# Attention scores: stores of 4 MB in 32 KB runs, 64-column matmul tiles, and eight small stores from 64 partitions

## The chip, the cores and the metric

The kernel runs on one core of a Trainium2 chip; the other cores of the chip run nothing of this program. The metric is the device time of one execution in microseconds (us). Times are medians of runs in the fast state unless said otherwise. "End" times inside a run are us from the start of the profiled span; the measured time is some 1.9 us longer than the span.

## The reference, cut to what matters

```python
def setup_inputs():
    batch, heads, seq, dim = 8, 8, 512, 64
    ... # q, k: float32 [8, 8, 512, 64]
def reference(q, k):
    scale = 1.0 / np.sqrt(q.shape[-1])
    return np.einsum('bhqd,bhkd->bhqk', q, k) * scale   # float32 [8, 8, 512, 512]
```

16.8 MB are read and 67.1 MB written, so this is a kernel that writes.

## The kernel before

A unit is two batches. Its inputs come in two loads of 2 MB, are cast to bf16, transposed on TensorE, and sorted into `kT` and `qz`. `qz` holds the stationary operand of two heads, zero where the other head's rows are, so one matmul of 128 rows and 128 columns makes 64 query rows of two heads. Eight query rows make a tile of 2 MB, 16 KB contiguous in memory for each partition:

```python
RO = 8
out_r = out.rearrange("(v b) (n h) (u i) k -> v (b n) (h u) (i k)", b=2, h=2, i=RO)
...
def scores(v, n):
    kT, qz = ts[v]
    o = out_pool.tile([P, RO, S], f32, name="o")            # 4 buffers
    for i in range(0, RO, 2):
        ps = psum_pool.tile([P, 2, S], f32, name="ps")
        for w in range(2):
            nc.tensor.matmul(out=ps[:, w, :], lhsT=qz[:, i + w, n, :], rhs=kT[:, n]..., ...)
        evacuate(o[:, i:i + 2, :], ps)                      # ScalarE and VectorE in turn
        yield
    nc.sync.dma_start(out=out_r[v, n], in_=o...)            # 32 of these
```

## Time and profile before

| | before |
|---|---|
| time, median of 4 runs | 204.16 us (204.10 to 204.36) |
| span of the profiled run | 202.3 us |
| data packets | 5120 of 16 KB |
| data queue busy, share of 16 DMA engines | 97.7% |
| landing marks of the last store, sixteen engines | mean 198.53 us, last 201.01 us |

Every DMA engine that takes part in a transfer writes one mark of 4 bytes when its share has landed, and the packet records of the trace show the sixteen marks of the last store. The kernel is over when the last of them is, so the mean tells how much work there was and the distance from the mean to the last tells how unevenly it ended. (The prediction reads the same marks from the semaphore's records, which lie about 0.5 us later.)

### The profile page before, as it was taken

How to read it: one execution, taken by the hardware profiler on the slowest of the kernel's cores; microseconds unless marked ns; L12 is line 12 of the kernel's file. 1: busy time of each engine (PE TensorE's matmuls, PEld its weight loads, DVE VectorE, ACT ScalarE, POOL GpSimd, SP SyncE). 2: the span in 40 equal slices, each digit the busy share in tenths (PEclk: the TensorE clock that was granted, in tenths of full speed). 3: DMA queues.
4: the chain of work that ended last, by engine and by line, in shares of the span. 5: the costliest groups of instructions: out<-in, count | busy, mean ns of one | idle time of the engine just before them, and what ended most of it. 6: DMA issues, size and time to landing. Idle time of an engine off the chain costs nothing.

```text
span 202.3 us, 1549 instructions
## 1 busy us (share of the span) xinstructions
PE 106.1 (52%) x512; PEld 50.2 (25%) x512; DVE 129.6 (64%) x133; ACT 102.5 (51%) x130; POOL 26.8 (13%) x20
## 2 busy tenths in 40 slices
PE   0045557755854755858575575656564677642000
PEld 0034424432211322423222233223121222210000
DVE  6875669987765686878787788777544455553000
ACT  2254457967654448484756666574833344442000
POOL 1037775756000000000000000000000000000000
PEclk9999999978799699797979787896969655695555
DMA  6999999999999999999999999999999999999991
GB/s 214 428 441 428 424 441 421 424 395 434 437 421 434 432 423 431 434 428 428 437 424 431 431 424 434 434 428 431 434 428 428 431 434 428 428 437 429 416 447 75
DMA packets 5768, 83.99 MB, mean 415 GB/s; under 512 B 640, under 2 KB 640, under 8 KB 640
## 3 DMA queue, kind: packets, MB, share of 16 engines
q1 hardware_dynamic: 5760, 83.89, 97.7%
q8 instruction: 4, 0.07, 0.1%
q14 instruction: 4, 0.03, 0.0%
HBM read 16.78 MB, written 67.11 MB: 415 GB/s over the span
## 4 chain that ended last, share of the span: by engine, by line
DMA 52%; ACT 13%; DVE 13%; PE 10%; issue 2%; ACTq 0%; DVEq 0%; SPq 0%
DMA out_dram<-o 52%; ACT o L62 6%; DVE o L64 5%; PE ps L134 5%; ACT qz L99 4%; DVE qz L89 3%; ACT kT L99 3%; PE tp L120 3%; DVE kT L99 3%; PE tp L111 2%; DVE xb L83 1%; DVE qz L99 1%; ACTq L62 0%; DVEq L64 0%; SPq L140 0%
## 5 line engine op out<-in xcount | busy, mean ns | idle before, releaser
L134 PE MATMUL ps<-kT,qz 128*128 128x512 bf16 x256 | 87.3, 470 | 52.4 <-ACT o L62 43.3
L64 DVE TENSOR_SCALAR o<-ps 128x1024 f32<-128x1024 f32 x64 | 78.2, 1225 | 44.1 <-DMA out_dram<-o 28.5
L62 ACT ACTIVATE o<-ps 128x1024 f32<-128x1024 f32 x64 | 63.5, 1022 | 64.3 <-DMA out_dram<-o 50.9
L134 PEld LDWEIGHTS <-qz 128*128 128x128 bf16 x256 | 28.6, 115 | 98.6 <-issue 87.2
L83 POOL CAST xb<-xf 128x2048 bf16<-128x2048 f32 x14 | 26.1, 1893 | 21.5 <-DMA xf<-in_q_dram 18.1
L99 DVE COPY kT<-tp 64x512 bf16<-64x512 bf16 x32 | 22.0, 687 | 4.3 <-PE tp L111 3.8
L99 DVE COPY qz<-tp 64x512 bf16<-64x512 bf16 x32 | 22.0, 687 | 4.2 <-PE tp L120 3.7
L111 PE MATMUL tp<-identity,xb 128*128 128x128 bf16 x128 | 13.0, 267 | 17.0 <-DVE xb L83 11.1
L99 ACT COPY kT<-tp 64x512 bf16<-64x512 bf16 x32 | 18.5, 578 | 5.0 <-PE tp L111 4.7
L99 ACT COPY qz<-tp 64x512 bf16<-64x512 bf16 x32 | 18.5, 577 | 4.2 <-PE tp L120 3.9
L120 PE MATMUL tp<-identity,xb 128*128 128x128 bf16 x128 | 13.3, 271 | 8.1 <-ACT qz L99 4.9
L111 PEld LDWEIGHTS <-xb 128*128 128x128 bf16 x128 | 11.2, 122 | 21.3 <-ACT xb L83 11.1
L120 PEld LDWEIGHTS <-xb 128*128 128x128 bf16 x128 | 11.5, 123 | 12.6 <-issue 9.7
L89 DVE MEMSET qz<- 64x2048 uint32 x4 | 7.1, 1765 | 2.6 <-issue 1.4
L83 ACT CAST xb<-xf 128x2048 bf16<-128x2048 f32 x1 | 1.9, 1898 | 6.7 <-DMA xf<-in_k_dram 6.7
L83 ACT ACT_TABLE_LOAD x1 | 1.3, 1283 | 0.7 <-PEq L181 0.7
L83 DVE CAST xb<-xf 128x2048 bf16<-128x2048 f32 x1 | 1.2, 1227 | 0.0
masks.py:199 POOL TENSOR_SCALAR_AFFINE_SELECT identity<-identity 128x128 bf16<-128x128 bf16 x1 | 0.3, 292 | 0.1
masks.py:197 POOL MEMSET identity<- 128x128 bf16 x1 | 0.2, 205 | 0.3 <-POOLq L181 0.3
L181 POOL MEMSET const-float32-0.0<- 128x1 f32 x1 | 0.1, 98 | 0.2 <-issue 0.2
L181 POOL MEMSET const-bfloat16-1.0<- 128x1 bf16 x1 | 0.1, 101 | 0.0
L181 POOL MEMSET const-uint8-127<- 128x1 uint8 x1 | 0.1, 101 | 0.0
(1 smaller groups left out, 0.1 us busy)
## 6 DMA issues: line engine op xcount, KB each, us to landing
out_dram<-o SPq DMA_DIRECT2D x32, 2048.0 KB, 16.1
xf<-in_k_dram SPq DMA_DIRECT2D x4, 2048.0 KB, 11.3
xf<-in_q_dram SPq DMA_DIRECT2D x4, 2048.0 KB, 12.3
```

Source lines behind the costliest of these rows:

```text
L62: pinned(nc.scalar.mul(out=dst, in_=src, mul=scale))
L64: pinned(nc.vector.tensor_scalar(out=dst, in0=src, scalar1=scale, scalar2=None, op0=mybir.AluOpType.mult))
L83: pinned(copy(out=xb[:, :, s, :], in_=xf[:, s].rearrange("p (j d) -> p j d", j=J)))
L89: nc.vector.memset(qz[half(h), :, :, (1 - h) * U:(2 - h) * U], 0.0)
L99: pinned(copy(out=dst(s, h), in_=src[:, h]))
L111: pinned(nc.tensor.transpose(out=tp[:, j, :], identity=identity, in_=kb[:, j0 + j].rearrange("p s d -> p (s d)")))
L120: pinned(nc.tensor.transpose(out=tp[:, i, jj, :], identity=identity, in_=qb[:, RO * jj + i0 + i].rearrange("p s d -> p (s d)")))
L134: pinned(nc.tensor.matmul(out=ps[:, w, :], lhsT=qz[:, i + w, n, :], rhs=kT[:, n].rearrange("d m s j -> d (m s j)"), start=True, stop=True))
L181: nc = _bacc.Bacc("TRN2", target_bir_lowering=False, num_devices=1)
```

## The change

The intent, as the design suggests: fewer and longer packets (32 KB instead of 16 KB), and an evening-out of the sixteen DMA engines at the end. A tile now holds 16 query rows, 4 MB, of four heads. A matmul now makes 64 output rows (two heads, 32 of them each), so two of them, in the two 64-column halves of TensorE's array, fill the 128 partitions. They are called split matmuls or column tiles below. Inputs and outputs share three buffers. Two of the sixteen rows of one tile are computed on partitions 0 to 63 instead and leave in eight small stores, each of 8 partitions.

```diff
-    RO = 8
+    RO = 16
+    out_r = out.rearrange("(v b) (t h) (u i) k -> v (b t) (h u) (i k)", b=2, h=4, i=RO)
+    out_l = out.rearrange("(v b) (t x h) (u i) k -> v (b t) (h u) x (i k)", b=2, x=2, h=2, i=RO)
-    raw_pool ... bufs=3          out_pool ... bufs=4
+    big_pool = ctx.enter_context(tc.tile_pool(name="big", bufs=3))
+    LOW = 2
+    low_at = (1, 0)
+    low = low_pool.tile([D, 2, LOW, S], f32, name="low")
...
+    def store_low(n):
+        p0 = 32 * (n // 4) + n % 4
+        p = slice(p0, p0 + 29, 4)
+        nc.sync.dma_start(out=out_l[low_at + (p, slice(None), slice((RO - LOW) * S, RO * S))],
+                          in_=low[p].rearrange("p x i k -> p x (i k)"))
...
+            if (v, t) == low_at and i == RO - LOW:
+                for x in range(2):
+                    ps = psum_pool.tile([P, 2, S], f32, name="ps")
+                    for w in range(2):
+                        matmul(v, t, i + w, x, ps[half(0), w, :])
+                    evacuate(low[:, x], ps[half(0)])
...
             for w in range(2):
+                for x in range(2):
+                    matmul(v, t, i + w, x, ps[half(x), w, :])
...
+        nc.sync.dma_start(out=out_r[v, t], in_=src)
+        since = (v - low_at[0]) * TILES + t - low_at[1] - 1
+        if 0 <= since < 8:
+            store_low(since)
```

Cut: the casts of the first unit move from VectorE and ScalarE to GpSimd, and the order in which transposes are mixed in changes.

More of the change, by code (lines that the diff above doesn't have):

```diff
@@ L36 @@
     IW = 8 // JJ
+    TILES = N // 2
     f32 = mybir.dt.float32
@@ L42 @@
     k_r = k.rearrange("(v b) g (m j) d -> v (b g m) (j d)", b=2, j=R)
-    out_r = out.rearrange("(v b) (n h) (u i) k -> v (b n) (h u) (i k)", b=2, h=2, i=RO)
+    out_r = out.rearrange("(v b) (t h) (u i) k -> v (b t) (h u) (i k)", b=2, h=4, i=RO)
+    out_l = out.rearrange("(v b) (t x h) (u i) k -> v (b t) (h u) x (i k)", b=2, x=2, h=2, i=RO)
     consts = ctx.enter_context(tc.tile_pool(name="consts", bufs=1))
-    raw_pool = ctx.enter_context(tc.tile_pool(name="raw", bufs=3))
-    bf_pool = ctx.enter_context(tc.tile_pool(name="bf", bufs=5))
+    big_pool = ctx.enter_context(tc.tile_pool(name="big", bufs=3))
+    bf_pool = ctx.enter_context(tc.tile_pool(name="bf", bufs=6))
     t_pool = ctx.enter_context(tc.tile_pool(name="t", bufs=2))
-    out_pool = ctx.enter_context(tc.tile_pool(name="out", bufs=4))
+    low_pool = ctx.enter_context(tc.tile_pool(name="low", bufs=1))
     tpsum_pool = ctx.enter_context(tc.tile_pool(name="tpsum", bufs=2, space=bass.MemoryType.PSUM))
@@ L60, in evacuate @@
         nonlocal n_evac
-        if n_evac % 2 == 0:
+        if n_evac % 6 in (0, 2, 3):
             pinned(nc.scalar.mul(out=dst, in_=src, mul=scale))
@@ L71, in load_and_cast @@
     def load_and_cast(v):
+        xf = big_pool.tile([P, 2, 2, J * D], f32, name="big")
         both = []
-        for src in (k_r, q_r):
-            xf = raw_pool.tile([P, 2, J * D], f32, name="xf")
-            nc.sync.dma_start(out=xf, in_=src[v])
+        for x, src in enumerate((k_r, q_r)):
+            nc.sync.dma_start(out=xf[:, x], in_=src[v].rearrange("p (s c) -> p s c", s=2))
+        for x in range(2):
             xb = bf_pool.tile([P, J, 2, D], bf16, name="xb")
             for s in range(2):
-                if v == 0 and src is k_r:
-                    copy = (nc.vector.tensor_copy, nc.scalar.copy)[s]
-                else:
-                    copy = nc.gpsimd.tensor_copy
-                pinned(copy(out=xb[:, :, s, :], in_=xf[:, s].rearrange("p (j d) -> p j d", j=J)))
+                pinned(nc.gpsimd.tensor_copy(out=xb[:, :, s, :],
+                                             in_=xf[:, x, s].rearrange("p (j d) -> p j d", j=J)))
             both.append(xb)
         return both
-    def clear(qz, h):
-        nc.vector.memset(qz[half(h), :, :, (1 - h) * U:(2 - h) * U], 0.0)
     def rearrange(tp, pattern, dst):
@@ L125, in transpose, with matmul, scores @@
                                  .rearrange("d i n (m s jj) -> d s i n m jj", s=2, jj=JJ)[:, s])
-    def scores(v, n):
+    def matmul(v, t, i, x, dst):
         kT, qz = ts[v]
-        o = out_pool.tile([P, RO, S], f32, name="o")
-        for i in range(0, RO, 2):
+        pinned(nc.tensor.matmul(out=dst, lhsT=qz[:, i, 2 * t + x, :],
+                                rhs=kT[:, 2 * t + x].rearrange("d m s j -> d (m s j)"),
+                                start=True, stop=True))
+    def store_low(n):
[3 more added lines that the diff above has]
+                          in_=low[p].rearrange("p x i k -> p x (i k)"))
+    def scores(v, t):
+        o = big_pool.tile([P, RO, S], f32, name="big")
+        for i in range(0, RO, 2):
+            if (v, t) == low_at and i == RO - LOW:
[4 more added lines that the diff above has]
+                    evacuate(low[:, x], ps[half(0)])
+                yield
+                break
             ps = psum_pool.tile([P, 2, S], f32, name="ps")
             for w in range(2):
-                pinned(nc.tensor.matmul(out=ps[:, w, :], lhsT=qz[:, i + w, n, :],
-                                        rhs=kT[:, n].rearrange("d m s j -> d (m s j)"),
-                                        start=True, stop=True))
+                for x in range(2):
+                    matmul(v, t, i + w, x, ps[half(x), w, :])
             evacuate(o[:, i:i + 2, :], ps)
@@ L139, in scores @@
         src = o.rearrange("p i k -> p (i k)")
-        nc.sync.dma_start(out=out_r[v, n], in_=src)
+        if (v, t) == low_at:
+            nc.sync.dma_start(out=out_r[v, t, :, :(RO - LOW) * S], in_=src[:, :(RO - LOW) * S])
+            return
+        nc.sync.dma_start(out=out_r[v, t], in_=src)
+        since = (v - low_at[0]) * TILES + t - low_at[1] - 1
+        if 0 <= since < 8:
+            store_low(since)
     def take(steps, count):
@@ L147 @@
     make_identity(nc, identity)
-    qzs = [consts.tile([P, RO, N, P], bf16, name=f"qz{n}") for n in range(2)]
+    qzs = [consts.tile([P, RO, N, 2 * U], bf16, name=f"qz{n}") for n in range(2)]
     for qz in qzs:
-        for h in range(2):
-            clear(qz, h)
+        nc.vector.memset(qz, 0.0)
     cast = [load_and_cast(v) for v in range(UNITS)]
@@ L158 @@
         ahead = transpose(v + 1, *cast[v + 1]) if v + 1 < UNITS else iter(())
-        per_step = 3 if v == 0 else 1
-        for n in range(N):
-            take(ahead, 1)
-            for _ in scores(v, n):
-                take(ahead, per_step)
+        for t in range(TILES):
+            for n, _ in enumerate(scores(v, t)):
+                take(ahead, 1 + (n % 4 == 3) if v else 2 * (t > 0))
         for _ in ahead:
```

## The prediction

> **What bounds the kernel now.** I read the page from the top. The busy line, the slices and the queue come first, because they tell whether any engine has to be argued about at all.
>
> ```profile
> PE 106.1 (52%) x512; PEld 50.2 (25%) x512; DVE 129.6 (64%) x133; ACT 102.5 (51%) x130; POOL 26.8 (13%) x20
> ...
> DMA  6999999999999999999999999999999999999991
> ...
> DMA packets 5768, 83.99 MB, mean 415 GB/s; under 512 B 640, under 2 KB 640, under 8 KB 640
> ...
> q1 hardware_dynamic: 5760, 83.89, 97.7%
> ```
>
> No compute engine is over 64%, while the DMA digits are 9 in 38 of 40 slices, and the data queue alone is busy for 97.7% of sixteen engines' span. So the end is set by bytes divided by rate, plus the two edges (the 6 in front, the 1 at the end). Of 5760 packets 640 are under 512 B: 40 transfers times 16, the marks of landing. The other 5120 carry 83.89 MB, so 16 KB each: one run of a partition. Their time is 0.977 x 202.3 x 16 / 5120 = 618 ns on average.
>
> Next the waits and the chain, to see whether the queue ever ran dry.
>
> ```profile
> ACT o L62 <- DMA out_dram<-o: 50.9, 24, 3.0
> PE ps L134 <- ACT o L62: 43.3, 29, 2.4
> DVE o L64 <- DMA out_dram<-o: 28.5, 24, 2.0
> ```
>
> ScalarE waits 50.9 us and VectorE 28.5 us for a store to free an output buffer: compute is ahead and is held back by the stores. The chain of waits calls 52% DMA; its ACT, DVE and PE pieces are only the refill of a buffer while other stores are already queued.
>
> Last the windows over both edges (columns after the engines: clock, DMA share, GB/s):
>
> ```profile
> 0.00:2.00 2.00, 0.00 (x0) 0.00 (x0) 0.78 (x1) 1.27 (x1) 0.70 (x6) 1.00 0.54 98
> 2.00:4.00 2.00, 0.00 (x0) 0.00 (x0) 1.53 (x2) 0.01 (x1) 0.00 (x0) 1.00 0.60 205
> ...
> 40.00:42.00 2.00, 0.61 (x3) 0.19 (x2) 1.96 (x3) 1.77 (x3) 2.00 (x2) 1.00 1.04 360
> ...
> 196.00:197.00 1.00, 0.00 (x0) 0.00 (x0) 0.00 (x0) 0.00 (x0) 0.00 (x0) 0.50 0.92 393
> 197.00:198.00 1.00, 0.00 (x0) 0.00 (x0) 0.00 (x0) 0.00 (x0) 0.00 (x0) 0.50 0.84 360
> 198.00:199.00 1.00, 0.00 (x0) 0.00 (x0) 0.00 (x0) 0.00 (x0) 0.00 (x0) 0.50 0.27 115
> 199.00:200.00 1.00, 0.00 (x0) 0.00 (x0) 0.00 (x0) 0.00 (x0) 0.00 (x0) 0.50 0.15 66
> 200.00:201.00 1.00, 0.00 (x0) 0.00 (x0) 0.00 (x0) 0.00 (x0) 0.00 (x0) 0.50 0.04 16
> ```
>
> The end is a taper of 4 us. The sixteen marks of the last store's landing in the trace say the same: nine lie at 197.98 to 198.41 us, then 198.98, 199.32, 199.37, 199.41, 199.54, 200.61 and 201.48. One engine works 3 us longer than most. The second loss is 40 to 42 us, where loads give way to stores: 360 instead of 430 GB/s, some 0.3 us.
>
> **What the Trainium skill says.** (1) "DMA: Bandwidth & Descriptors", section "Why small descriptors are slow (HBM only)": a packet costs its 32-byte beats plus about 3 cycles. The trace agrees in size only: a 2 MB transfer takes about 2.097 MB / 430 GB/s = 4.88 us, 8 packets for each engine, and no larger packet is there to compare. (2) Same page, "The descriptor swizzle": in a transfer of 128 partitions, engines 0 to 7 serve partitions 0 to 63 and engines 8 to 15 the others. This profile does not tell engines apart. (3) Same page, "Why a DMA increments its semaphore by 16 and not by 1": a transfer whose slowest dimension is 8 goes to the lowest-numbered 8 engines. No run here shows it yet. (4) "TensorE: Matmul & The Clock Gate", Part 3: matmuls whose outputs lie in different column groups run at the same time; 3 such tiles were measured at 2.38 times. The kernel before has none.
>
> **The change, part by part.**
>
> *Longer runs.* 32 stores of 2 MB become 15 of 4 MB, one of 3.5 MB and 8 of 64 KB. Per engine the stores were 256 packets of 16 KB and become about 128 of 32 KB. By (1), 3 of 515 cycles are overhead in a 16 KB packet (512 beats + 3) and 3 of 1027 in a 32 KB one, a gain of 0.29%. Stores are 67.1 MB / 430 GB/s = 156 us, so an estimate of 0.45 us. There are also 8 full-width store marks fewer on engines 0 to 7 and 16 fewer on engines 8 to 15 (the 8 small stores use only half the engines); a mark took 9 ns in the packet records, so 0.1 us. Together 0.5 to 0.6 us, on the bound.
>
> *The small stores.* Two of 16 rows of one 4 MB tile are 512 KB. Stored in full width they would be 32 KB for each engine. They are moved to partitions 0 to 63 and stored 8 partitions at a time, so by (2) and (3) engines 0 to 7 take 64 KB each and the others none. Engines 8 to 15 lose 32 KB, engines 0 to 7 gain 32 KB: at 611 ns for 16 KB (the median packet) 1.2 us each way. If the late seven are among engines 8 to 15, which I take from the design of the change, the latest goes from 201.48 to about 200.3, and the early eight from at most 198.4 to 199.7: the end is 1.2 us earlier. A perfect levelling could give some 2.7 us (spread the shares after 197 evenly: the work is done near 198.2 instead of 201).
>
> *TensorE.* 256 matmuls of 128 columns become 512 of 64. In the trace, starts of 128x512 matmuls lie 0.427 us apart at half clock and 0.215 at full. If a pair overlaps, nothing changes (about 110 us). If it does not, a 4 MB tile takes 32 x 0.215 = 6.9 us at full clock plus two transpose groups of 0.5 us: 7.9 us, still below the 9.75 us of its store; at half clock 13.7 + 2 would exceed it[...].
>
> *VectorE and ScalarE.* The same 64 + 64 evictions in all but 2 of half height; ScalarE gets half as before. The transposes' copies stay 64 and 64. Per unit of 16 MB of output VectorE needs 16 x 1.225 + 16 x 0.687 = 30.6 us against 39 us of store: beside the path.
>
> *Buffers.* Inputs and outputs now share three buffers of 32 KB a partition. A tile fills in about 8 us, and may begin when the store three back has landed, while two more (19.5 us) are queued: 9 us of slack even with 2 to 3 us of late landing. The danger is the first tile. It takes the buffer of unit 1, whose casts on GpSimd (1.89 us each, all 16 there now) end about 4 x 0.93 us after its q lands: loads land 4.9 us apart from 8.7, so q of unit 1 at 23.4, free at 27.1. Transposes of unit 0 start 1.4 us later than before (GpSimd casts its k: 8.7 + 3.7 = 12.4 instead of 11.05), so the first matmul moves from 28.7 to about 29.5. Eight evictions at 0.86 us (half clock, pairs overlapping) end near 37.5, and the queue is full of loads until about 42: the store comes 3 to 4 us in time. No gap.
>
> **Sum.** 204.17 - 1.2 - 0.6 = 202.4; 202.3 with a little for fewer, longer packets in the crossing of loads and stores.
>
> **The rivals.** (a) *The pairs of matmuls run one after the other.* For it: both tiles use all 128 rows. Against: (4), and the 2 us per tile in hand. Result: first store up to 2 us late at worst, 202.5 to 205; only with half clock throughout some 16 x 15.7 + 30, about 280 us. (b) *The late engines are not 8 to 15.* The trace's late engine falls behind through single packets of 1 to 1.9 us at 33 and 42 us, which may hit another engine in another order; then up to 1.2 us is added to a late engine: 204.5 to 205. (c) *32 KB runs are cut to 16 KB, or the marks and packets are hidden anyway.* Then only the levelling stays: 203. (d) *A gap between loads and stores* because three shared buffers start the first tile later than I reckon: each us of gap is a us of time. Three to four us in hand speak against it.
>
> **Range and chances.** All gains live in 83.89 MB's 195 us and its edges. Full levelling and the whole 0.6 us would give 200.8; a gain over 2% needs below 200.1, so levelling plus a faster steady rate: chance 0.08. Slower by 2%, above 208.3, needs rival (a) at half clock or a gap of 4 us or more: 0.06. Range 200.5 to 204.4.
>
> **What would show each step.** Packets of 32 KB, about 2050 of them, with a median near 1.21 us or a little less than twice the old one; windows of full share at 430 to 432 GB/s between 45 and 195 us; a taper at the end shorter than 3 us; no slice under 9 near 40 us; matmul pairs starting close together. Wrong would be: a dip of the DMA share in mid-span, waits of SyncE's stores for evictions that leave the queue empty, or a taper as long as before with other marks late.

## More of the kernel before

Another line, which the prediction did not use, is that of the second DMA queue in the page's list of queues (packets, MB, share):

```profile
q8 instruction: 4, 0.07, 0.1%
```

These are four packets of 16 KB that bring instructions while the kernel runs.

## The result, and the profile after

| | before | after |
|---|---|---|
| time, median of 4 runs | 204.16 us | 205.24 us (205.11 to 205.42) |
| ratio, 95% interval | | 1.0051 (1.0034 to 1.0069) |
| last store's marks: mean | 198.53 | 198.01 |
| last store's marks: last | 201.01 | 202.18 |

A ratio is the mean time of one kernel's fast runs over that of the other's of the same rounds, so it is not quite the ratio of the two medians. The change is 1.1 us slower, within 2%, and outside the predicted range. The mean of the marks fell by 0.5 us: there is a little less work. The last mark rose by 1.2 us: it ends less evenly. The page after (busy time of engines, DMA slices, packets, queues):

```profile
PE 106.6 (52%) x768; PEld 56.1 (28%) x768; DVE 126.3 (62%) x130; ACT 101.9 (50%) x130; POOL 30.5 (15%) x22
...
DMA  6999999999999999999999999999999999999970
...
DMA packets 3656, 84.00 MB, mean 413 GB/s; under 512 B 448, under 2 KB 448, under 8 KB 576
...
q1 hardware_dynamic: 3648, 83.89, 96.5%
q8 instruction: 6, 0.10, 0.2%
```

No compute engine comes near the length of the run: TensorE is busy for 106.6 us (106.1 before), its weight loads for 56.1 (50.2), and GpSimd, with the moved casts, for 30.5 (26.8). The middle is as full as before, and the last two slices read 7 and 0 instead of 9 and 1. 3648 packets are 1920 of 32 KB, 128 of 28 KB, 1024 loads of 16 KB, 128 small ones of 4 KB, and 448 marks: 24 x 16 + 8 x 8, so a small store really ran on 8 engines. The instruction queue has 6 packets, not 4. Over the tail (windows; the last three columns are clock, DMA share, GB/s):

```profile
196.00:197.00 1.00, 0.00 (x0) 0.00 (x0) 0.00 (x0) 0.00 (x0) 0.00 (x0) 0.50 0.68 295
197.00:198.00 1.00, 0.00 (x0) 0.00 (x0) 0.00 (x0) 0.00 (x0) 0.00 (x0) 0.50 0.53 229
198.00:199.00 1.00, 0.00 (x0) 0.00 (x0) 0.00 (x0) 0.00 (x0) 0.00 (x0) 0.50 0.23 98
199.00:200.00 1.00, 0.00 (x0) 0.00 (x0) 0.00 (x0) 0.00 (x0) 0.00 (x0) 0.50 0.08 33
200.00:201.00 1.00, 0.00 (x0) 0.00 (x0) 0.00 (x0) 0.00 (x0) 0.00 (x0) 0.50 0.08 33
```

A packet is counted in the window in which it starts. Before (these lines are in the prediction), the share fell from 0.84 to 0.27 within one us; now it thins out for longer, with single packets at 199.75 and 200.96. The taper was to become shorter and became longer: the sixteen marks lie between 195.84 and 202.18 us (before: 197.62 and 201.01). In the waits, the compute side is as the prediction says (line: waiting, for whom, us, times, longest):

```profile
ACT big L72 <- PE ps L134: 29.5, 26, 2.9
DVE big L74 <- DMA out_dram<-big: 25.5, 9, 4.3
ACT big L72 <- DMA out_dram<-big: 23.4, 10, 4.4
```

Evictions wait for stores to land, 48.9 us together, so stores still bind. And the groups of instructions show that the split matmuls overlap, 512 of them in less busy time than 256 had (before, then after; the number behind the bar is the busy time):

```profile
L134 PE MATMUL ps<-kT,qz 128*128 128x512 bf16 x256 | 87.3, 470 | 52.4 <-ACT o L62 43.3
...
L134 PE MATMUL ps<-kT,qz 128*64 128x512 bf16 x512 | 85.0, 458 | 49.4 <-ACT big L72 37.0
```

In the trace the two matmuls of nearly every pair start within some 60 ns of each other, most within 30, and pairs follow each other at 0.215 us at full clock. The first store was issued at 36.10 us, and the last packet of the loads started at 43.1, so no gap opened there.

### The profile page after: what moved, and what is told of

The parts are those of the page before. It is cut to its first block, busy times and chain, and to the rows that moved or that the text cites. A ratio compares the mean times of both kernels' runs of the same rounds, so it can differ in the third digit from the quotient of the medians.

```text
span 203.5 us, 1985 instructions
## 1 busy us (share of the span) xinstructions
PE 106.6 (52%) x768; PEld 56.1 (28%) x768; DVE 126.3 (62%) x130; ACT 101.9 (50%) x130; POOL 30.5 (15%) x22
## 3 DMA queue, kind: packets, MB, share of 16 engines
q1 hardware_dynamic: 3648, 83.89, 96.5%
## 4 chain that ended last, share of the span: by engine, by line
DMA 42%; DVE 7%; PE 7%; ACT 5%; issue 1%; ACTq 0%; DVEq 0%; SPq 0%
DMA out_dram<-big 42%; PE ps L134 6%; DVE big L74 5%; ACT big L72 4%; DVE qz L103 2%; ACT qz L103 1%; PE tp L115 0%; ACT kT L103 0%; PE tp L124 0%; ACTq L72 0%; DVEq L74 0%; SPq L167 0%
## 5 line engine op out<-in xcount | busy, mean ns | idle before, releaser
L134 PE MATMUL ps<-kT,qz 128*64 128x512 bf16 x512 | 85.0, 458 | 49.4 <-ACT big L72 37.0
L74 DVE TENSOR_SCALAR big<-ps 128x1024 f32<-128x1024 f32 x63 | 75.4, 1220 | 38.6 <-DMA out_dram<-big 25.5
L72 ACT ACTIVATE big<-ps 128x1024 f32<-128x1024 f32 x64 | 64.1, 1022 | 58.3 <-PE ps L134 29.5
L134 PEld LDWEIGHTS <-qz 128*64 128x64 bf16 x512 | 36.8, 125 | 86.8 <-issue 75.3
L90 POOL CAST xb<-big 128x2048 bf16<-128x2048 f32 x16 | 29.8, 1893 | 16.8 <-DMA big<-in_k_dram 11.8
L115 PE MATMUL tp<-identity,xb 128*128 128x128 bf16 x128 | 11.6, 249 | 15.0 <-POOL xb L90 12.4
L124 PE MATMUL tp<-identity,xb 128*128 128x128 bf16 x128 | 12.8, 265 | 7.4 <-ACT qz L103 3.6
L115 PEld LDWEIGHTS <-xb 128*128 128x128 bf16 x128 | 9.1, 112 | 20.5 <-POOL xb L90 12.4
L124 PEld LDWEIGHTS <-xb 128*128 128x128 bf16 x128 | 10.2, 120 | 14.6 <-issue 14.3
L180 DVE MEMSET qz<- 128x4096 uint32 x2 | 6.9, 3472 | 2.5 <-PEq L208 1.7
L74 DVE TENSOR_SCALAR low<-ps 64x1024 f32<-64x1024 f32 x1 | 1.2, 1217 | 0.7 <-PE ps L134 0.7
L72 ACT ACTIVATE low<-ps 64x1024 f32<-64x1024 f32 x1 | 1.0, 1017 | 0.0
```

The source lines that it names most:

```text
L72: pinned(nc.scalar.mul(out=dst, in_=src, mul=scale))
L74: pinned(nc.vector.tensor_scalar(out=dst, in0=src, scalar1=scale, scalar2=None, op0=mybir.AluOpType.mult))
L90: pinned(nc.gpsimd.tensor_copy(out=xb[:, :, s, :], in_=xf[:, x, s].rearrange("p (j d) -> p j d", j=J)))
L115: pinned(nc.tensor.transpose(out=tp[:, j, :], identity=identity, in_=kb[:, j0 + j].rearrange("p s d -> p (s d)")))
L124: pinned(nc.tensor.transpose(out=tp[:, i, jj, :], identity=identity, in_=qb[:, RO * jj + i0 + i].rearrange("p s d -> p (s d)")))
L134: pinned(nc.tensor.matmul(out=dst, lhsT=qz[:, i, 2 * t + x, :], rhs=kT[:, 2 * t + x].rearrange("d m s j -> d (m s j)"), start=True, stop=T ...
```

## The experiments

**Theory A**: the small stores load the wrong half of the engines. In the records of the changed kernel the eight marks of a small store follow 0.33 us (two packets of 4 KB) behind eight of the sixteen marks of the store before it, and the two latest are among those eight. **Theory B**: the small stores level as intended, and runs, buffers or split matmuls cost the time. All kernels gave correct results. Ratios are to the kernel before on the same chip, timed alternately.

### 1. Without the small stores

```diff
-    low_at = (1, 0)
+    low_at = (-9, 0)      # never: all sixteen tiles are stored whole
```

> The changed kernel without the small stores: all sixteen 4 MB tiles stored whole, in 32 KB runs. Theory A (the small stores load the wrong half: the landing marks of the changed kernel show that the eight engines which take them include the two latest ones): the latest engine loses 8 x 0.33 us of small packets and gets back 1.2 us of its own share, so about 1.5 us or more less than the changed kernel: 202.5 to 203.8 us, below the kernel before (ratio to it 0.992 to 0.998). Theory B (32 KB runs, shared buffers or the split matmuls cost the time and the small stores level as intended): up to 1.2 us more than the changed kernel, 205.2 to 206.5, ratio 1.005 to 1.012.

Measured: 203.87 us (203.66 to 204.08), ratio 0.9983 (0.9970 to 0.9995). That is 1.4 us less than the changed kernel; the last mark is at 200.88 instead of 202.18, with the same mean, 198.01. Theory B falls. The time lies just above theory A's range. The rest of the change is a gain, though a small one. Its tail:

```profile
196.00:197.00 1.00, 0.00 (x0) 0.00 (x0) 0.00 (x0) 0.00 (x0) 0.00 (x0) 0.50 0.76 328
197.00:198.00 1.00, 0.00 (x0) 0.00 (x0) 0.00 (x0) 0.00 (x0) 0.00 (x0) 0.50 0.46 197
198.00:199.00 1.00, 0.00 (x0) 0.00 (x0) 0.00 (x0) 0.00 (x0) 0.00 (x0) 0.50 0.15 66
199.00:200.00 1.00, 0.00 (x0) 0.00 (x0) 0.00 (x0) 0.00 (x0) 0.00 (x0) 0.50 0.08 33
200.00:201.00 1.00, 0.00 (x0) 0.00 (x0) 0.00 (x0) 0.00 (x0) 0.00 (x0) 0.50 0.00 0
```

The packet that started after 200 us is gone.

### 2. Only the small stores, on the kernel before

```diff
+            evacuate(low if (v, n) == low_at and i == RO - 2 else o[:, i:i + 2, :], ps)
...
+        if 0 <= since < 16:          # sixteen stores of 8 partitions x 4 KB, one behind each store
+            nc.sync.dma_start(out=out_r[low_at + (p, slice((RO - 2) * S, RO * S))], in_=low[p]...)
```

> The kernel before, with only the small stores added: two of eight rows of one 2 MB tile (512 KB) go out in sixteen stores of 8 partitions, the rest as before in 16 KB runs with whole matmuls. Theory A (engines 0 to 7 hold the latest engine, here too): the latest engine gets 32 KB more, 1.2 us plus small packets, so 205.3 to 206.5, ratio 1.005 to 1.012. Theory B (the small stores level as intended): about 1.2 us less than before, 203.0, ratio 0.994.

Measured: 205.49 us, ratio 1.0068 (1.0054 to 1.0082). The small stores alone cost 1.3 us here as well, as theory A says. Not all of it is their place: the mean of the marks rose too, from 198.53 to 199.40, which theory A does not explain. These stores take 4 KB from each of the 128 partitions, eight partitions at a time, and more packets than usual are lengthened between 45 and 183 us in this run. So this run alone would not settle it.

### 3. Runs of 16 KB in the new tiles

```diff
-        nc.sync.dma_start(out=out_r[v, t], in_=src)
+        for c in (slice(0, RO * S // 2), slice(RO * S // 2, RO * S)):
+            nc.sync.dma_start(out=out_r[v, t, :, c], in_=src[:, c])
```

> As e1_plain, but each 4 MB tile goes out in two stores of 8 rows, so in runs of 16 KB again. Theory A with the term for longer runs as predicted: 0.5 to 0.6 us more than e1_plain. If run length does nothing: the same as e1_plain within 0.2 us. If 32 KB runs cost time (theory B): 0.5 us or more less than e1_plain.

Measured: 205.06 us, ratio 1.0048 (1.0035 to 1.0061), 1.2 us more than with 32 KB runs, where 0.5 to 0.6 was expected. The mean of the marks is 198.70 against 198.01, so the saved work is 0.7 us, and the last engine gained more than the mean (1.2 us in its mark; why is not shown). The packet records give the first figure: a 16 KB packet takes 611 ns, a 32 KB packet 1213, and in both cases the next one starts 3 ns before the end. So 32 KB take 2 x 608 = 1216 ns in the one form and 1210 in the other, and 6 ns x 128 is 0.77 us.

### 4. Only the split matmuls, on the kernel before

```diff
+                for x in range(2):
+                    nc.tensor.matmul(out=ps[half(x), w, :], lhsT=qz[:, i + w, n, half(x)], ...)
```

> The kernel before with each score matmul cut into two of 64 columns and nothing else: 768 instead of 512 matmuls on TensorE. Theory A: stores bind, so the same as before within 0.3 us; the trace should show two more 16 KB fetches of instructions (6 instead of 4), each taking a DMA engine some 0.9 us, and where one hits the engine that ends last up to 0.9 us more (204.1 to 205.1). Theory C (the split matmuls bind TensorE): waits of the evictions for TensorE grow and the time rises by over 1 us.

Measured: 205.18 us, ratio 1.0050 (1.0037 to 1.0062): 1.0 us for the same arithmetic with 512 more instructions (256 matmuls and 256 weight loads), although stores bind. That is just above the expected range. The last mark is at 202.19 instead of 201.01, the mean only 0.27 later (198.80). The instruction queue has 6 packets, as expected. Theory C, that TensorE binds, falls: the evictions' waits for TensorE did not grow (before, then this run):

```profile
DVE o L64 <- PE ps L134: 15.1, 22, 1.9
ACT o L62 <- PE ps L134: 13.1, 9, 2.9
...
DVE o L64 <- PE ps L135: 14.7, 24, 1.3
ACT o L62 <- PE ps L135: 9.8, 8, 2.9
```

### 5. Is it the column tiles, or the number of instructions?

```diff
-            for j in range(8):
-                transpose(out=tp[:, j, :], in_=kb[:, j0 + j]...)
+            for j in range(16):
+                transpose(out=tp[:, j // 2, :], in_=kb[:, j0 + j // 2]...)    # q likewise
```

> The kernel before with every transpose on TensorE issued twice into the same place: 768 matmuls as in the split version, but no 64-column tiles and no change of any store. Theory D (it is the number of TensorE's instructions that costs: 16 KB fetches of them take a DMA engine each, 0.9 us and more): six fetches instead of four, all sixteen engines later by about 0.1 to 0.3 us on average, the last by up to 1.2 us, 204.6 to 205.4, as in e4_pe64 (205.18). Rival C (the 64-column matmuls themselves cost the 1.0 us of e4_pe64): as before, 204.0 to 204.4.

Measured: 204.81 us, ratio 1.0037 (1.0023 to 1.0051), last mark 201.62, mean 198.68. Without any column tile, 256 useless matmuls and their weight loads cost 0.8 us. Rival C falls, at least for most of the 1.0 us. How extra instructions reach the stores is less clear. The 16 KB fetches are there, 0.88 to 1.0 us each:

```profile
q1 hardware_dynamic: 5760, 83.89, 97.3%
q8 instruction: 6, 0.10, 0.2%
q14 instruction: 4, 0.03, 0.0%
```

But another thing in the packet records fits the sizes better. In every kernel, some packets between 45 and 183 us are lengthened by 7 to 100 ns; in the version of experiment 1 they follow one another without a gap, so they lie on one DMA engine, and eighteen packets of ordinary length behind the last of them lead exactly to the last mark at 200.88. None of the five fetches in that stretch lies on that engine: its packets run on, one behind the other, while each fetch is under way. Their lengthening sums to 2.8 us in the kernel before (1549 instructions), 3.9 in experiment 4 (2061), 3.4 in experiment 5 (2061) and 3.7 in experiment 1 (1976). Against the kernel before that is +1.1 and +0.5 us, where the last marks moved by +1.2 and +0.6. So the engine that ends last is, in experiment 1 for certain, slowed by about 3% while instructions run, and by something else than the fetches; and the sums suggest that more instructions slow it more (experiment 3, with 2008, fits too: 3.7 us, and a last mark 1.0 us later than before). In the other runs the records do not let its packets be followed through. What shares that engine was not found: no record of the trace names it. All timed runs also recorded their span and clock, so whether it is there without any recording is open too.

### 6. Which engine ends last?

```diff
+    for n in range(2, 16):       # behind the last store
+        probe = consts.tile([n, 16 * n], f32, name=f"probe{n}")
+        nc.sync.dma_start(out=probe, in_=k_r[0][0:n, 0:16 * n])
```

By the rule that the prediction cites under (3), a tiny load of n rows runs on the n lowest-numbered engines; its packets have 64 n bytes, and the trace has n of them for each n. So the first tiny packet behind an engine's last mark names the engine: 320 bytes is n = 5, the first that reaches engine 4. The number 4 rests on that rule; the order in which engines join is in the trace.

> The kernel before with a ladder of fourteen tiny loads behind the last store: the n-th has n rows of 64 n bytes (n = 2 to 15), so by the Trainium skill's rule it runs on the n lowest-numbered DMA engines, and the size of the first tiny packet on an engine tells its number. A marker, not a change: some 1 us or more longer at the end. Theory A: the engine that ends its stores last is among 0 to 7 (its first tiny packet is of 512 bytes or less). Theory B: the late ones are 8 to 15 (first tiny packet of 576 bytes or more, or none).

> The changed kernel without the small stores, with the same ladder behind the last store. Theory A: the engine that ends its stores last is among 0 to 7, so the small stores add to it. Theory B: it is among 8 to 15, and the small stores relieve it.

> The changed kernel with the ladder of tiny loads behind the last store. Theory A: engine 4 ends last, near 202.2 us, engines 8 to 15 end 2 to 6 us ahead of it (195.8 to 197.5); a marker, the total some 4 us longer. Theory B: the last is among 8 to 15.

Measured, from the packet records (the ladder lengthens the runs to 208.17, 207.74 and 209.56 us; single runs, state unknown, used for the order only):

```
last store's mark, us           before    without small    changed
engine 4 (next packet 320 B)    201.14        200.69         202.03
engine 5 (next packet 384 B)    199.00        199.29         200.04
engines 8 to 15, last           199.83        198.33         197.36
```

Engine 4 ends last in all three, in the half that the small stores load. (In the kernel before, some of the other late ones did lie among 8 to 15.) With them engines 8 to 15 finish 1.0 us sooner, and engine 4 finishes 1.3 us later.

### 7. The small stores from GpSimd

```diff
-        nc.sync.dma_start(out=out_l[...], in_=low[p]...)
+        nc.gpsimd.dma_start(out=pad, in_=k_r[0][0:8, 0:32]...)          # second: these two swapped
+        nc.gpsimd.dma_start(out=out_l[...], in_=low[p]...)
```

> The changed kernel with its eight small stores issued from GpSimd instead of SyncE, each behind a tiny load of 8 rows. By the Trainium skill, a transfer of 8 from GpSimd takes 8 consecutive engines from a cursor that goes round, so the tiny loads take engines 0 to 7 and the stores 8 to 15. Theory A: engine 4, the last one (at 200.9 us in the version without small stores), loses 32 KB = 1.2 us, engines 8 to 15 (at most 198.3 there) get 1.2 us and the small packets: the last ends near 199.7 to 200.0, so 202.7 to 203.1 us, ratio 0.993 to 0.995, the fastest of all. If where the small stores run does not matter: as the changed kernel, 205.2.

> The same instructions as e7_pool_second with one difference: each small store stands ahead of its tiny load, so the stores take engines 0 to 7 and the loads 8 to 15. Theory A: like the changed kernel, 204.9 to 205.6, some 2 us more than e7_pool_second. If it is the issuing from GpSimd that matters, or the cursor does not go round so: the same as e7_pool_second.

Measured: 204.53 us, ratio 1.0018 (1.0006 to 1.0031), and 204.40 us, ratio 1.0013 (0.9999 to 1.0027). Both expectations missed: the order made no difference, and neither beat the version without small stores. The means of the marks rose to 198.83 and 199.11, so stores from GpSimd cost work of their own. On which engines they ran the records do not tell. This attempt is inconclusive on theory A.

### 8. The same bytes on four or eight engines, first attempt

Instead of splitting the tile by rows over the whole width, the last two rows of partitions 0 to 63 (256 KB) went to small stores and the rest left in one store of partitions 0 to 63 and one of 64 to 127.

```diff
+            nc.sync.dma_start(out=out_r[v, t, half(0), :(RO - LOW) * S], in_=src[half(0), :(RO - LOW) * S])
+            nc.sync.dma_start(out=out_r[v, t, half(1)], in_=src[half(1)])
```

> The version without small stores, with 256 KB of one tile (two rows of partitions 0 to 63) moved to small stores of 4 partitions, which by the Trainium skill run on engines 0 to 3 only. Theory A (engine 4 ends last, so what counts is whether it is among those that take the small stores): engines 4 to 15 lose 16 KB = 0.6 us, engines 0 to 3, which end at 197 to 197.7 us without them, get 48 KB = 1.8 us and stay below 200. The last ends 0.6 us earlier than in e1_plain: 203.1 to 203.5 us, ratio 0.995 to 0.997. Rival E (any small store costs, wherever it runs): 0.5 us or more above e1_plain, 204.4.

> The same 256 KB from the same partitions in the same packets of 4 KB, in small stores of 8 partitions, so on engines 0 to 7. Theory A: engine 4 gets 16 KB more, 0.6 us and 0.1 for marks: 204.4 to 204.8, ratio 1.001 to 1.003, over 1 us more than e9_four. Rival E: like e9_four or less, as there are half as many stores.

Measured: 213.63 us (211.29 to 214.66) and 213.33 us (210.56 to 214.93), medians of all six runs, of which one and two were slow; the ratios of the fast runs are 1.0446 and 1.0397. Neither theory allowed for this. The windows of the first show where it went (the last two columns are DMA share and GB/s):

```profile
80.00:85.00 5.00, 3.10 (x24) 1.33 (x21) 4.96 (x6) 3.17 (x5) 0.00 (x0) 0.83 1.08 302
85.00:90.00 5.00, 4.00 (x30) 1.88 (x28) 3.95 (x6) 3.13 (x5) 0.00 (x0) 0.83 0.98 238
90.00:95.00 5.00, 2.19 (x20) 1.14 (x20) 1.72 (x2) 2.56 (x4) 0.00 (x0) 1.00 1.03 210
95.00:100.00 5.00, 0.00 (x0) 0.00 (x0) 0.00 (x0) 0.00 (x0) 0.00 (x0) 0.69 0.88 288
100.00:105.00 5.00, 3.42 (x20) 1.76 (x21) 4.42 (x6) 2.05 (x2) 0.00 (x0) 0.50 1.02 439
```

The engines are busy all along, but at half the rate: a store of 64 partitions moves about 210 GB/s, its 28 KB packets take up to 2.45 us where 1.06 is usual. The Trainium skill, "SBUF — State Buffer", section "Door 1: The DMA port swizzle (why `[64,N]` ≈ `[32,N]`)", says that bandwidth depends on how many of 16 memory ports the partitions reach; partitions 0 to 63 reach 8 of them, and the 210 GB/s agree. The two stores hold 3.9 MB, 9 us at 430 GB/s and 18 at half of it; the 9 us between are about the loss. So the pair says nothing about theory A.

### 9. The same bytes on four or eight engines, second attempt

The changed kernel with one row instead of two on partitions 0 to 63 (256 KB), the rest in one whole-width store, and small stores of 4 or of 8 partitions:

```diff
-    LOW = 2
+    LOW = 1
+    FEW = 4                                # the other: FEW = 8
...
+        for f in range(8 // FEW):
+            p0 = 32 * (n // 4) + n % 4 + 4 * FEW * f
+            p = slice(p0, p0 + 4 * FEW - 3, 4)
+            nc.sync.dma_start(out=out_l[...], in_=low[p]...)
```

> The changed kernel with one row instead of two (256 KB) computed on partitions 0 to 63, and its small stores cut to 4 partitions, which should run on engines 0 to 3 only. Theory A (what counts is whether engine 4, the last, takes a share): engines 4 to 15 lose 16 KB = 0.6 us against e1_plain, engines 0 to 3 get 48 KB = 1.8 us and some 0.4 us for 2 KB packets and marks, and stay under 200. The last ends 0.6 us before that of e1_plain: 203.1 to 203.6 us, ratio 0.995 to 0.997. Rival E (small stores cost as such): twice as many of them as in e12_eight, so no faster than it, 204.4 or more.

> The same as e11_four with small stores of 8 partitions, so on engines 0 to 7. Theory A: engine 4 gets 16 KB more, 0.6 us, and 0.2 for small packets and marks: 204.4 to 204.9 us, ratio 1.001 to 1.004, 1.0 us or more above e11_four. Rival E: as e11_four or less.

Measured: 203.38 us (203.30 to 203.53), ratio 0.9966 (0.9953 to 0.9980), and 204.56 us (204.44 to 204.96), ratio 1.0024 (1.0011 to 1.0036). Same bytes, same partitions, same packets, twice as many stores in the first: 1.2 us faster when engines 4 to 7 do not take part. Both times lie in theory A's ranges, and rival E falls. The tails of the first and then of the second:

```profile
196.00:197.00 1.00, 0.00 (x0) 0.00 (x0) 0.00 (x0) 0.00 (x0) 0.00 (x0) 0.50 0.84 360
197.00:198.00 1.00, 0.00 (x0) 0.00 (x0) 0.00 (x0) 0.00 (x0) 0.00 (x0) 0.50 0.31 131
198.00:199.00 1.00, 0.00 (x0) 0.00 (x0) 0.00 (x0) 0.00 (x0) 0.00 (x0) 0.50 0.15 66
199.00:200.00 1.00, 0.00 (x0) 0.00 (x0) 0.00 (x0) 0.00 (x0) 0.00 (x0) 0.50 0.08 33
200.00:201.00 1.00, 0.00 (x0) 0.00 (x0) 0.00 (x0) 0.00 (x0) 0.00 (x0) 0.50 0.00 0
...
199.00:200.00 1.00, 0.00 (x0) 0.00 (x0) 0.00 (x0) 0.00 (x0) 0.00 (x0) 0.50 0.08 33
200.00:201.00 1.00, 0.00 (x0) 0.00 (x0) 0.00 (x0) 0.00 (x0) 0.00 (x0) 0.50 0.08 33
```

The first ends at 200.22 (last mark), and its span is 201.5 us; the second, in its profiled run, at 201.85. The first is the fastest version, faster than both kernels, by 0.3% against the one before.

### The account

| from | to | what differs | time, us | change | last mark |
|---|---|---|---|---|---|
| before | experiment 4 | split matmuls, 512 more instructions | 204.15 → 205.18 | +1.0 | 201.01 → 202.19 |
| experiment 4 | experiment 3 | 4 MB tiles, shared buffers, casts; runs still 16 KB | 205.18 → 205.06 | -0.1 | → 202.05 |
| experiment 3 | experiment 1 | runs of 32 KB | 205.06 → 203.87 | -1.2 | → 200.88 |
| experiment 1 | changed kernel | small stores, 512 KB on engines 0 to 7 | 203.87 → 205.24 | +1.4 | → 202.18 |

The dose fits as well: no small stores 203.87, 256 KB on eight engines 204.56, 512 KB on eight engines 205.24.

## Why the prediction was wrong, by its own steps

- **What bounds: right.** The DMA engines stayed full until the tail in every version (in experiment 8 for a while at half the rate), and the end was set by the latest of sixteen engines.
- **Longer runs: right mechanism, size too small.** Foreseen 0.5 to 0.6 us; measured (experiment 3) 0.7 us of work per engine and 1.2 us at the end. The saved piece is 6 ns in 1216, 0.5%, not the 0.29% worked out from the Trainium skill's 3 cycles a packet ("DMA: Bandwidth & Descriptors", "Why small descriptors are slow (HBM only)"). The 8 and 16 marks that were saved took 9 ns each, as said.
- **The small stores: the step that failed.** The prediction says "If the late seven are among engines 8 to 15, which I take from the design of the change". It foresaw -1.2 us and the runs show +1.4. How they were split over the engines was right (8 marks each, engines 0 to 7, engines 8 to 15 ended sooner). Where the late engines lie was an assumption with no view behind it, and it was wrong for the one that counts: the last is engine 4 (experiment 6), though some of the others were among 8 to 15. Taking engine 4 out of the small stores turned +0.7 us into -0.5 against the version without them (experiment 9). This is rival (b), which the prediction priced at 204.5 to 205 and then left out of its range. The reason that it gave for (b), single long packets at 33 and 42 us (1.05 to 1.6 us in the trace), is not what was found: where engine 4 could be followed, it lost its time in many packets lengthened by less than 0.1 us between 45 and 183 us.
- **TensorE: right on overlap, wrong on the bill.** Pairs start together, and TensorE's busy time hardly grew (106.1 to 106.6 us). That "nothing changes" was wrong: 512 more instructions cost 1.0 us (experiment 4), 0.8 of it without any column tile (experiment 5). No term of the sum held this, and its path to the late engine is not settled.
- **Buffers and the first tile: right.** The first score matmul started at 26.9 us (29.5 foreseen) and the first store was issued at 36.1 us (37.5 foreseen), no slice near 40 us fell below 9, and experiments 3 and 4 differ by 0.1 us for all of it.
- **The sum.** 202.3 was foreseen and 205.24 measured, 2.9 us more: 2.6 from the small stores (+1.4 in place of -1.2) and 1.0 from the instructions, less 0.6 from longer runs and 0.1 from the rest. That these terms close is no check of its own, as they are steps of one ladder from the kernel before to the changed one; experiments 2, 5 and 9 are the checks from outside it.

## What to carry to other kernels

In this kernel, bound by DMA for its whole length, the latest of the sixteen DMA engines decided here, not the mean. Before shifting load between engines, find out which is late, by tiny transfers of known width behind the last one, and then shift it away from that engine. Instructions on an engine that does not bind are not free in such a kernel: 512 of them cost 0.8 to 1.0 us here. If a large store has to be split, cut the bytes of each partition, as in experiment 3, and not the partitions into halves: stores of 64 partitions ran at half the rate here (experiment 8).

## What the Trainium skill lacked or had wrong

- No page has that engine 4 runs behind in a kernel whose transfers come from SyncE (the engines that the skill calls slower are 7 and 15, with a guess that ties it to GpSimd's transfers): engine 4 in three kernels here, one run each (last marks at 200.7 to 202.0 us, those of all others by 199.3 to 200.0), with packets about 3% longer while instructions run in the kernel where they could be followed.
- "Runtime: NRT & Kernel Launch", "Instruction fetch mechanics": a 16 KB block of instructions comes by DMA and crossing into it is "mostly hidden". The fetches agree (4 for 1024 and 6 for 1536 matmuls and weight loads), but each held a DMA engine 0.88 to 1.1 us, and the data packet behind it took some 0.4 us longer in most cases; 512 more instructions came with 0.8 to 1.0 us more time in a DMA-bound kernel. In the version of experiment 1 no fetch after 45 us fell on the engine that ended last, so there the fetches are not what made it late; for the others it is open.
- "DMA: Bandwidth & Descriptors", "Why small descriptors are slow (HBM only)": the gain from 16 KB to 32 KB packets was 0.5% (6 ns in 1216), 1.7 times what 3 cycles a packet give (0.29%).
- The same page, "Why a DMA increments its semaphore by 16 and not by 1": the lowest-numbered k engines for SyncE's transfers agree with experiments 6 and 9. Its cursor for transfers from GpSimd could not be shown: both orders of experiment 7 took the same time (204.5 and 204.4 us).
